# A two-layer diffusion backbone with product-key experts: scores issued one projection later, the shared bank's block fourth, five row buffers, fewer held activations, two adaLN groups moved between the layers

## The chip, the cores and the metric

The kernel runs on one core of one Trainium2 chip. The metric is the device time of one execution in microseconds; less is better. TensorE (PE in the profile) does the matrix products, with its weight loads shown apart as PEld; VectorE is DVE, ScalarE is ACT, GpSimd is POOL, and SyncE (SP) issues the plain DMAs. GpSimd issues the indirect DMAs, the gathers.

## What is computed

Latent tokens x (512 x 1024) and context tokens (256 x 1024) go through two layers. Each layer is three mixers side by side, a merge, and then an expert step (PEER) that picks 16 of 16384 experts for each of 8 heads of each token. Cut to what matters here:

```python
for l in range(2):
    mod = (silu(c) @ w_ada[l] + b_ada[l])          # adaLN: six rows of 1024 each
    h = modulate(rmsnorm(x, norm1_g[l]), mod[0], mod[1])
    q, k, v, zu, zv, zf, gl = split_cols(h @ w_in[l])
    x = x + mod[2] * mixer_merge(attention(q, k, v), chunk_mlp(zu, zv), fourier_mix(zf), gl, ...)
    h2 = modulate(rmsnorm(x, norm2_g[l]), mod[3], mod[4])
    x = x + mod[5] * peer_ffn(h2, ...)             # the context tokens alike in layer 0

def peer_ffn(t, w_q, sub_keys, u_tab, v_tab):
    q = rms_unit(t @ w_q)                          # 8 heads x 2 halves
    s = einsum('thpc,hpkc->thpk', q, sub_keys)     # key scores, 128 per half
    # top 16 of each half, of their 256 sums the top 16: idx (8 x 16 experts), weights g
    act = gelu(einsum('td,thkd->thk', t, u_tab[idx]))
    return einsum('thk,thkd->td', g * act, v_tab[idx])
```

## The kernel before

All data are float32. A product is made of three PE passes (`mm3`, lines 113 to 115): each operand is split into a high and a low half (ACT writes the high half at L102, DVE or POOL the low one at L109), and high times high, low times high and high times low are summed.

The expert step is done in two ways. **Dense**, for the 512 latent tokens of layer 0 and 384 of layer 1: all 16384 experts are computed in 128 chunks of 128 experts. `dense_u` multiplies a chunk of the u table (tile wH, wL) with the tokens into a PSUM bank du; a gelu on ACT (L972) puts the result into a held tile gS, or into DRAM (`gsd`) for chunks that are "spilled" and loaded back as gSr. `dense_v` loads the chunk of the v table (`vr`, by SP, three buffers with the tag vraw), splits it (vH, vL), multiplies gS by a table of gates (gt, L997), splits that (AH, AL) and multiplies it with eight 128-column blocks of v. Seven blocks accumulate over all chunks in PSUM banks da_0 to da_6. The eighth has no bank left: its product d goes into the one bank with the tag s, which du uses too, and DVE adds it to a tile da_7 in SBUF (L1013). A later du can start when this add has read the bank; d can start when gelu has read the du before it. NGSS says how many gS tiles are held, SPILL how many chunks go through DRAM. As many du as fit are made before the v chunks begin (`ahead`), the rest between them (`between`), one for each gS tile that comes free.

**Sparse**, for the two context blocks of layer 0 (128 tokens each) and the fourth latent block of layer 1: per block 128 gathers of rows of the u table (a job u), then 128 of the v table (a job v). A gather is issued by POOL (L869) into a tile `row` of a ring of LAG+1 = 4 buffers; `use` puts the work on DVE three steps later: for u a product with the tokens hn with its sum into dots (L888), for v a multiply-add into acc (L897). hn and acc share a buffer, so a u job loads hn (L887) after the acc of the job before has been stored. Steps are placed in the instruction stream by PE columns already issued (STEPS), so the jobs run beside the dense phase: in this trace c0 u from about 964 us, c0 v from 1694, c1 u from 2069, c1 v from 2501 to 2959 us. POOL also makes the wL halves of the u table.

At the end of layer 0 the eight da banks are scaled by mod, added to the residual (`xr`, four loads of 512 KB through the vraw buffers), stored (`xfin`), and their squares summed (vS); a product with ones (L294), a short chain on DVE (L172 to L181), a spread by a diagonal (dg, L299 and L305) and a copy (rf, L1282) give the norm factor with which layer 1 begins.

The adaLN rows are made by `ada` in groups: per group four loads `araw` (512 KB), 32 PE instructions as the trace counts them (L252), a copy, a small product and an add into mod. Groups 6 to 9 of layer 1 run beside its mixers.

`route1` makes the query of each head in two projections (tile pq), sums of squares (psq), the scores against the keys (pse) and the top 16 of them on DVE. The Tile framework's scheduler sets the order of the instructions on each engine.

Of the kernel before, what the change touches and what calls it, by code (L numbers as in the profile page):

```python
# [10 lines left out]
F32 = mybir.dt.float32  # L11
# [4 lines left out]
AF = mybir.ActivationFunctionType  # L16
# [5 lines left out]
P = 128  # L22
DEPTH = 2
D = 1024
# [7 lines left out]
NK = 128  # L32
# [16 lines left out]
LAG = 3  # L49
NGSS = (16, 30)  # L50
SPILL = ((40, 3), (40, 3))
FILL = (1.0, 1.3)
LEAD = 2
ADA = 6
# [23 lines left out]
class Ker:  # L78
# [156 lines left out]

    def ada(self, l, ccs, pool=None, tag="tl"):

        nc = self.nc
        sm, mod = self.lay[l]["sm"], self.lay[l]["mod"]
        p, nr = (pool, 4) if pool else (self.wp, self.wr)  # L240
        HW = 256
        for cc in ccs:
            acc = self.ps(tag)[:, :HW]
            for kk in range(4):
                raw = p.tile([P, D], F32, tag="wraw", name=self.nm("araw"), bufs=nr)
                nc.sync.dma_start(raw, self.a["wada"][l, cc, kk])
                self.spend()
                for j in range(2):
                    for hf in range(2):
                        q = 32 * (2 * j + hf)  # L250
                        c = j * 512 + hf * HW
                        nc.tensor.matmul(acc[q:q + 32, :], self.csil[:, 2 * kk + j, :], raw[:, c:c + HW],  # L252
                                         start=(kk == 0), stop=(kk == 3), skip_group_check=True)
                if tag == "fl" and kk < 3:
                    yield
            row = self.cp.tile([P, HW], F32, tag="row", name=self.nm("adar"), bufs=1)
            nc.scalar.activation(row, acc, AF.Copy)
            tp = self.ps(tag)
            for b in range(2):
# [336 lines left out]
    def merge_end(self, tmp, l, s, tag, e="alt"):  # L596
# [15 lines left out]
        for d in range(KD):  # L612
# [6 lines left out]
            yield  # L619
        nc.scalar.activation(s.r, self.rms(tmp, S, 1.0 / D, T), AF.Copy)  # L620

# [93 lines left out]
    def route1(self, l, tmp, rp, s, own=None):  # L715
# [5 lines left out]
        ss = rp.tile([P, nb, 16], F32, name=self.nm("pss"))  # L721
        self.rt = (V, I, ss)
        for h in range(HEADS):
            qs = []
            keys = tmp.tile([P, 2, NK], F32, tag="keys", name=self.nm("keys"), bufs=2)
            nc.sync.dma_start(keys, self.a["keys"][l, h])
            sp = self.ps("tl")
            for p in range(2):
                acc, = self.projT(l, W_PQ + 2 * h + p, [s], "pool", "px", own)
                q = tmp.tile([P, T], F32, tag=f"q{p}", name=self.nm("pq"), bufs=2)  # L730
                nc.scalar.activation(q, acc, AF.Copy)
                sq = tmp.tile([P, T], F32, tag="sq", name=self.nm("psq"), bufs=2)
                nc.scalar.activation(sq, acc, AF.Square)
                for b in range(nb):
                    nc.tensor.matmul(sp[:, 2 * b + p:2 * b + p + 1], sq[:, b * P:(b + 1) * P], self.onescol, start=True, stop=True)
                qs.append(q)
            nc.scalar.activation(ss[:, :, 2 * h:2 * h + 2], sp[:, :2 * nb].rearrange("p (a b) -> p a b", b=2), AF.Copy)
            for b in range(nb):
                sc = self.ps("tl")
                for p in range(2):  # L740
                    nc.tensor.matmul(sc[:, p * P:(p + 1) * P], qs[p][:, b * P:(b + 1) * P], keys[:, p, :], start=True, stop=True)
                sk = tmp.tile([P, 2, NK], F32, tag="s", name=self.nm("pse"), bufs=3)
                nc.scalar.activation(sk.rearrange("p a b -> p (a b)"), sc[:, :2 * P], AF.Copy)
                for p in range(2):
                    hp = 2 * h + p
                    s2 = tmp.tile([P, NK], F32, tag="s2", name=self.nm("ps2"), bufs=2)
                    self.top16(sk[:, p, :], s2, V[b][:, hp, :], I[b][:, hp, :])
            yield

    def route2(self, tmp, order, res, l=None):  # L750
# [106 lines left out]
    def step(self):  # L857
# [5 lines left out]
        if self.jobs:  # L863
            job = self.jobs[0]
            r, j, gp = job["r"], job["next"], self.gp
            if j == 0 and job["tab"] == "u":
                r["dots"] = gp.tile([P, P], F32, tag="dots", name=self.nm("dots"), bufs=2)
            row = gp.tile([P, D], F32, tag="row", name=self.nm("row"), bufs=LAG + 1)
            nc.gpsimd.indirect_dma_start(  # L869
# [107 lines left out]
    def dense_v(self, l, c, vp, sp, gS, gd, accs, acc7, between):  # L977
# [25 lines left out]
        def block(out, d, start, stop):  # L1003
            ds = slice(d * P, (d + 1) * P)
            self.mm3(out, vH[:, ds], vL[:, ds], AH, AL, start, stop)
        for d in range(4):
            block(accs[d], d, c == 0, c == NK - 1)
# [6 lines left out]
        self.added[c] = add.ins  # L1014
        for d in range(4, 7):
            block(accs[d], d, c == 0, c == NK - 1)
# [5 lines left out]
    def layer(self, l, xin, cin, xfin, rin):  # L1022
# [74 lines left out]
        with ExitStack() as e:  # L1097
# [10 lines left out]
            def context():  # L1108
# [4 lines left out]
                with ExitStack() as e2:  # L1113
                    tmp = self.pool(e2, f"cr{l}", side="right")
                    for b, r in enumerate(rc):
# [3 lines left out]
            self.interleave((mix(), 1), (context() if last else None, 1), (self.gates(gp, l, ss, (2, 1), PE2[l]), GATES[l]),  # L1119
                            (self.ada(l, range(ADA, 10) if last else range(4, 12), None, "fl"), 4 * AD[l]))  # L1120
            kvp = self.pool(ekv, f"kv{l}", side="right")
# [127 lines left out]
        with ExitStack() as e:  # L1249
            vp = self.pool(e, f"dv{l}")  # L1250
            acc7 = vp.tile([P, TD], F32, name=f"da{l}_7")
            with ExitStack() as e2:
# [11 lines left out]
                for c in range(NK):  # L1264
                    room[0] += not self.spilled(l, c)
                    self.dense_v(l, c, vp, op, gSs[c], gd, accs, acc7, between)
                known = not last and TD == SEQ
                if known:
                    S = vp.tile([P, SEQ], F32, tag="gSr", name=self.nm("vS"), bufs=2)
# [159 lines left out]
```

## Time and profile before

| | |
|---|---|
| median of 3 runs | 4845.99 us (4843.63 to 4858.48) |
| the profiled execution | 4854.88 us |
| its span in the profile | 4852.8 us |
| PE busy | 4484.0 us (92%) |
| DVE busy | 3251.8 us (67%) |
| POOL busy | 1794.6 us (37%) |
| mean granted clock of PE | 0.963 of full speed |

The span is the time from the first to the last instruction of the profiled execution; 2.1 us of that execution lie around it. Busy time is summed over stages that have different limits, so a change is read in its own stretch of the span.

### The profile page before, as it was taken

The numbers are of one execution on the slowest core, as the hardware profiler recorded it, in microseconds if no ns is written. First come the engines' busy times: TensorE is split into PE (matmuls) and PEld (weight loads), VectorE is DVE, ScalarE is ACT, GpSimd is POOL, SyncE is SP. The second block draws the span as 40 slices with busy tenths as digits, with TensorE's granted clock in tenths as the row PEclk, the third lists the DMA queues.
The fourth block names the chain that finished last, engine by engine and source line by source line (L and its number), as shares of the span: only waits on it lengthen the run. The fifth ranks groups of instructions, "written<-read, shape, count | busy, mean of one in ns | idle before, by whom it ended". The sixth has DMA issues, their size and how long they took to land.

```text
span 4852.8 us, 64913 instructions
## 1 busy us (share of the span) xinstructions
PE 4484.0 (92%) x23501; PEld 3843.0 (79%) x23501; DVE 3251.8 (67%) x6538; ACT 1872.6 (39%) x3456; POOL 1794.6 (37%) x1114
## 2 busy tenths in 40 slices
PE   7899988889889999999899989989898999999998
PEld 5678877767678788877778767767787899999998
DVE  3115586868996577766677874457459966777787
ACT  2223454333678322222222333334334883333332
POOL 1111012335323566655556420110224335555531
PEclk9999999989999999999999999999999999999999
DMA  4442345557768898988789886333536788888986
GB/s 167 137 145 78 95 124 171 179 187 229 238 237 283 291 316 307 319 274 281 264 299 305 308 270 206 97 102 108 176 89 197 265 280 282 293 290 301 309 281 227
DMA packets 447504, 1092.81 MB, mean 225 GB/s; under 512 B 37200, under 2 KB 193744, under 8 KB 440016
## 3 DMA queue, kind: packets, MB, share of 16 engines
q1 hardware_dynamic: 336592, 685.97, 43.4%
q0 software_dynamic: 110592, 402.70, 24.2%
q8 instruction: 185, 3.03, 0.3%
q14 instruction: 135, 1.11, 0.1%
HBM read 970.04 MB, written 118.49 MB: 224 GB/s over the span
## 4 chain that ended last, share of the span: by engine, by line
PE 43%; DMA 6%; DVE 6%; issue 6%; POOL 4%; ACT 1%; POOLq 0%; DVEq 0%; SPq 0%; ACTq 0%
PE da L114 5%; PE da L115 5%; PE da L113 5%; PE du L113 5%; PE du L115 5%; PE du L114 5%; POOL row L869 3%; DMA row<-in_u_dram,idxc 2%; PE ps L114 2%; PE ps L113 2%; PE ps L115 2%; PE px L952 1%; POOL wL L109 1%; DVE row L888 1%; PE d L113 1%
## 5 line engine op out<-in xcount | busy, mean ns | idle before, releaser
L109 POOL TENSOR_TENSOR wL<-wraw,wH 128x1024 fp32r<-128x1024 f32 x291 | 722.0, 2483 | 1138.5 <-ACT wH L102 1033.7
L102 ACT ACTIVATE wH<-wraw 128x1024 fp32r<-128x1024 f32 x460 | 486.7, 1059 | 1124.9 <-issue 311.1
L113 PE MATMUL du<-dH,wH 128*128 128x512 f32 (+1 forms) x2048 | 780.7, 381 | 71.3 <-DVE da L1013 47.2
L115 PE MATMUL du<-dH,wL 128*128 128x512 f32 (+1 forms) x2048 | 771.4, 377 | 44.6 <-DVE wL L109 24.4
L114 PE MATMUL du<-dL,wH 128*128 128x512 f32 (+1 forms) x2048 | 768.4, 375 | 2.4 <-DVE dL L336 2.4
L113 PE MATMUL da<-AH,vH 128*128 128x512 f32 (+1 forms) x1792 | 646.4, 363 | 7.0 <-ACT AH L102 7.0
L114 PE MATMUL da<-AL,vH 128*128 128x512 f32 (+1 forms) x1792 | 650.4, 363 | 1.4 <-DVE AL L109 1.2
L115 PE MATMUL da<-AH,vL 128*128 128x512 f32 (+1 forms) x1792 | 649.3, 362 | 0.0
L888 DVE SCALAR_TENSOR_TENSOR row<-row,hn 128x1024 f32<-128x1024 f32 x384 | 502.7, 1329 | 110.4 <-DMA row<-in_u_dram,idxc 93.4
L102 ACT ACTIVATE vH<-vr 128x1024 fp32r<-128x1024 f32 x256 | 271.8, 1062 | 776.8 <-PE da L114 552.7
L869 POOL DMA_INDIRECT row<-in_u_dram,idxc x256 | 329.4, 1287 | 528.9 <-DVE row L888 441.2
L897 DVE SCALAR_TENSOR_TENSOR acc<-row,dots,acc 128x1024 f32<-128x1024 f32 x381 | 502.0, 1318 | 10.0 <-DMA row<-in_v_dram,idxc 6.1
L113 PEld LDWEIGHTS du<-dH,wH 128*128 128x128 f32 x2048 | 399.4, 195 | 132.4 <-DVE da L1013 57.0
L869 POOL DMA_INDIRECT row<-in_v_dram,idxc x256 | 337.6, 1319 | 393.2 <-DVE acc L897 350.7
L115 PEld LDWEIGHTS du<-dH,wL 128*128 128x128 f32 x2048 | 398.7, 195 | 96.6 <-DVE wL L109 28.7
L114 PEld LDWEIGHTS du<-dL,wH 128*128 128x128 f32 x2048 | 399.3, 195 | 42.3 <-DVE dL L336 2.9
L1013 DVE TENSOR_TENSOR da<-d,da 128x512 f32<-128x512 f32 (+1 forms) x254 | 158.1, 623 | 333.4 <-PE d L115 333.0
L109 DVE TENSOR_TENSOR wL<-wraw,wH 128x1024 fp32r<-128x1024 f32 x169 | 213.9, 1266 | 249.4 <-ACT wH L102 220.3
L113 PEld LDWEIGHTS da<-AH,vH 128*128 128x128 f32 x1792 | 337.3, 188 | 43.3 <-ACT AH L102 8.2
L114 PEld LDWEIGHTS da<-AL,vH 128*128 128x128 f32 x1792 | 337.4, 188 | 39.0 <-DVE AL L109 4.2
L115 PEld LDWEIGHTS da<-AH,vL 128*128 128x128 f32 x1792 | 337.4, 188 | 35.0
L109 DVE TENSOR_TENSOR vL<-vr,vH 128x1024 fp32r<-128x1024 f32 x256 | 326.2, 1274 | 50.9 <-ACT vH L102 49.2
(390 smaller groups left out, 8968.1 us busy)
## 6 DMA issues: line engine op xcount, KB each, us to landing
wraw<-in_uT_dram SPq DMA_DIRECT2D x256, 512.0 KB, 4.6
vr<-in_v_dram SPq DMA_DIRECT2D x256, 512.0 KB, 6.2
wraw<-in_wt_dram SPq DMA_DIRECT2D x204, 512.0 KB, 3.9
gd<-stg SPq DMA_DIRECT2D x56, 1024.0 KB, 6.3
araw<-in_wada_dram SPq DMA_DIRECT2D x96, 512.0 KB, 4.6
gt<-gd SPq DMA_DIRECT2D x16, 2048.0 KB, 17.9
gt<-gd SPq DMA_DIRECT2D x16, 1536.0 KB, 12.3
gatex<-g SPq DMA_DIRECT2D x48, 256.0 KB, 2.1
```

The source lines that it names most:

```text
L102: nc.scalar.activation(H, src, AF.Copy)
L109: e.tensor_tensor(L, src, H.bitcast(F32), op=ALU.subtract)
L113: nc.tensor.matmul(out, aH, bH, start=start, stop=False)
L114: nc.tensor.matmul(out, aH, bL, start=False, stop=False)
L115: nc.tensor.matmul(out, aL, bH, start=False, stop=stop)
L869: nc.gpsimd.indirect_dma_start(out=row, out_offset=None, in_=self.a[f"{job['tab']}{job['l']}"], in_offset=bass.IndirectOffsetOnAxis(ap=r[" ...
L888: nc.vector.scalar_tensor_tensor(row, row, 1.0, job["hn"], op0=ALU.mult, op1=ALU.mult, accum_out=dots[:, j:j + 1])
L897: nc.vector.scalar_tensor_tensor(job["acc"], row, dots[:, j:j + 1], job["acc"], op0=ALU.mult, op1=ALU.add)
L952: nc.tensor.matmul(gp3[:, :, j], ob[:, j, :], oa[:, j, :], start=True, stop=True)
L1013: add = nc.vector.tensor_tensor(acc7, s[:, :TD], acc7, op=ALU.add)
```

## The change

- `NGSS` falls from 16 to 14 (layer 0) and from 30 to 27 (layer 1); `SPILL` rises from 40 to 42 chunks in both layers.
- The ring of row buffers grows from 4 to 5.
- In `dense_v` the block d is issued as the fourth of the eight instead of the fifth.
- adaLN groups 6 and 7 of layer 1 are no longer made beside layer 1's mixers, but at the end of layer 0's dense phase, ahead of the residual's loads, through the three vraw buffers and the one bank s.
- `merge_end` yields twice more and issues the two halves of the norm factor apart.
- In `route1` the sums, scores and top 16 of a head are issued after the first projection of the next head; one copy serves two token blocks.

```diff
-NGSS = (16, 30)
-SPILL = ((40, 3), (40, 3))
+NGSS = (14, 27)
+SPILL = ((42, 3), (42, 3))
...
-    def ada(self, l, ccs, pool=None, tag="tl"):
+    def ada(self, l, ccs, pool=None, tag="tl", ps=None, raws=("wraw", 4)):
...
-        p, nr = (pool, 4) if pool else (self.wp, self.wr)
+        p, rt, nr = (pool, *raws) if pool else (self.wp, "wraw", self.wr)
+        ps = ps or (lambda: self.ps(tag))
...
-            acc = self.ps(tag)[:, :HW]
+            acc = ps()[:, :HW]
...
-                raw = p.tile([P, D], F32, tag="wraw", name=self.nm("araw"), bufs=nr)
+                raw = p.tile([P, D], F32, tag=rt, name=self.nm("araw"), bufs=nr)
...
-        nc.scalar.activation(s.r, self.rms(tmp, S, 1.0 / D, T), AF.Copy)
+        yield
+        dg = self.rmsd(tmp, S, 1.0 / D, T)
+        yield
+        nc.scalar.activation(s.r, self.spread(dg, T), AF.Copy)
...
+        def best(h, keys, qs, sqs):
+
+            sp = self.ps("tl")
+            for p in range(2):
+                for b in range(nb):
+                    nc.tensor.matmul(sp[:, 2 * b + p:2 * b + p + 1], sqs[p][:, b * P:(b + 1) * P], self.onescol, start=True, stop=True)
+            nc.scalar.activation(ss[:, :, 2 * h:2 * h + 2], sp[:, :2 * nb].rearrange("p (a b) -> p a b", b=2), AF.Copy)
+            for b0 in range(0, nb, 2):
+                sc = self.ps("tl")
+                for j in range(2):
+                    for p in range(2):
+                        o = (2 * j + p) * P
+                        nc.tensor.matmul(sc[:, o:o + P], qs[p][:, (b0 + j) * P:(b0 + j + 1) * P], keys[:, p, :], start=True, stop=True)
+                sk = tmp.tile([P, 2, 2, NK], F32, tag="s", name=self.nm("pse"), bufs=2)
+                nc.scalar.activation(sk.rearrange("p j a b -> p (j a b)"), sc, AF.Copy)
...
                 acc, = self.projT(l, W_PQ + 2 * h + p, [s], "pool", "px", own)
+                if p == 0 and last is not None:
+                    best(*last)
...
-            row = gp.tile([P, D], F32, tag="row", name=self.nm("row"), bufs=LAG + 1)
+            row = gp.tile([P, D], F32, tag="row", name=self.nm("row"), bufs=LAG + 2)
...
-        for d in range(4):
+        for d in range(3):
             block(accs[d], d, c == 0, c == NK - 1)
         s = sp.tile([P, 512], F32, tag="s", name=self.nm("d7"))
         block(s[:, :TD], 7, True, True)
...
-        for d in range(4, 7):
+        for d in range(3, 7):
             block(accs[d], d, c == 0, c == NK - 1)
...
-                            (self.ada(l, range(ADA, 10) if last else range(4, 12), None, "fl"), 4 * AD[l]))
+                            (self.ada(l, range(ADA + 2, 10) if last else range(4, 12), None, "fl"), 4 * AD[l]))
...
+                shared = lambda: op.tile([P, 512], F32, tag="s", name=self.nm("s"))
+                if not last:
+                    self.drain(self.ada(l + 1, range(ADA, ADA + 2), vp, "tl", shared, ("vraw", 3)))
```

On PE, in one chunk of layer 0's dense phase, before (a number at the end of a name tells one tile from the next; the blocks are da_0 to da_6, the shared bank's block is d):

```order
L115 MATMUL da_2_14607<-AH_17984,vL_17978 128x512
L113 MATMUL da_3_14608<-AH_17984,vH_17977 128x512
L114 MATMUL da_3_14608<-AL_17985,vH_17977 128x512
L115 MATMUL da_3_14608<-AH_17984,vL_17978 128x512
L113 MATMUL d_3348_18000<-AH_17984,vH_17977 128x512
L114 MATMUL d_3348_18000<-AL_17985,vH_17977 128x512
L115 MATMUL d_3348_18000<-AH_17984,vL_17978 128x512
L113 MATMUL da_4_14609<-AH_17984,vH_17977 128x512
L114 MATMUL da_4_14609<-AL_17985,vH_17977 128x512
```

The same place after the change:

```order
L113 MATMUL da_2_14531<-AH_17953,vH_17948 128x512
L114 MATMUL da_2_14531<-AL_17954,vH_17948 128x512
L115 MATMUL da_2_14531<-AH_17953,vL_17949 128x512
L113 MATMUL d_3314_18005<-AH_17953,vH_17948 128x512
L114 MATMUL d_3314_18005<-AL_17954,vH_17948 128x512
L115 MATMUL d_3314_18005<-AH_17953,vL_17949 128x512
L113 MATMUL da_3_14532<-AH_17953,vH_17948 128x512
L114 MATMUL da_3_14532<-AL_17954,vH_17948 128x512
L115 MATMUL da_3_14532<-AH_17953,vL_17949 128x512
```

The three passes of d stand ahead of those of da_3, so three blocks lie between a chunk's du and d, and four between d and the next du.

On SP, at the end of layer 0, before:

```order
L985 DMA vr_23000<-in_v_dram 128x1024
L1272 DMA xr_23044<-xm_88 128x1024
L1272 DMA xr_23053<-xm_88 128x1024
L1272 DMA xr_23064<-xm_88 128x1024
L1278 DMA xfin_87<-xr_23044 128x1024
L1278 DMA xfin_87<-xr_23053 128x1024
L1272 DMA xr_23075<-xm_88 128x1024
L324 DMA nx_23168<-xfin_87 128x512
L324 DMA nx_23174<-xfin_87 128x512
```

After the change:

```order
L1003 DMA vr_22925<-in_v_dram 128x1024
L247 DMA araw_22969<-in_wada_dram 128x1024
L247 DMA araw_22975<-in_wada_dram 128x1024
L247 DMA araw_22981<-in_wada_dram 128x1024
L247 DMA araw_22987<-in_wada_dram 128x1024
L247 DMA araw_23001<-in_wada_dram 128x1024
L247 DMA araw_23007<-in_wada_dram 128x1024
L247 DMA araw_23013<-in_wada_dram 128x1024
L247 DMA araw_23019<-in_wada_dram 128x1024
L1293 DMA xr_23033<-xm_88 128x1024
L1293 DMA xr_23042<-xm_88 128x1024
L1293 DMA xr_23053<-xm_88 128x1024
```

Eight loads araw stand between the last load of the v table and the first residual load xr; all of them use the three buffers with the tag vraw in turn.

On DVE, in job c1 u beside the dense phase, before (a use is a row with hn; da_7 is the add that frees the shared bank):

```order
L109 TENSOR_TENSOR AL_18735<-gS_17105,AH_18734 128x512
L888 SCALAR_TENSOR_TENSOR row_18698,dots_17798<-row_18698,hn_17870 128x1024
L888 SCALAR_TENSOR_TENSOR row_18711,dots_17798<-row_18711,hn_17870 128x1024
L888 SCALAR_TENSOR_TENSOR row_18724,dots_17798<-row_18724,hn_17870 128x1024
L1013 TENSOR_TENSOR da_7_14601<-d_3480_18707,da_7_14601 128x512
L888 SCALAR_TENSOR_TENSOR row_18687,dots_17798<-row_18687,hn_17870 128x1024
L997 TENSOR_TENSOR gSr_18815<-gSr_18815,gt_18598 128x512
L109 TENSOR_TENSOR vL_18812<-vr_18809,vH_18811 128x1024
L109 TENSOR_TENSOR AL_18819<-gSr_18815,AH_18818 128x512
L1013 TENSOR_TENSOR da_7_14601<-d_3495_18789,da_7_14601 128x512
L888 SCALAR_TENSOR_TENSOR row_18769,dots_17798<-row_18769,hn_17870 128x1024
```

After the change, in the same job:

```order
L1031 TENSOR_TENSOR da_7_14525<-d_3445_18710,da_7_14525 128x512
L906 SCALAR_TENSOR_TENSOR row_18648,dots_17781<-row_18648,hn_17817 128x1024
L906 SCALAR_TENSOR_TENSOR row_18693,dots_17781<-row_18693,hn_17817 128x1024
L1015 TENSOR_TENSOR gS_17362<-gS_17362,gt_18522 128x512
L109 TENSOR_TENSOR vL_18778<-vr_18775,vH_18777 128x1024
L109 TENSOR_TENSOR AL_18783<-gS_17362,AH_18782 128x512
L906 SCALAR_TENSOR_TENSOR row_18718,dots_17781<-row_18718,hn_17817 128x1024
L1031 TENSOR_TENSOR da_7_14525<-d_3454_18755,da_7_14525 128x512
L906 SCALAR_TENSOR_TENSOR row_18704,dots_17781<-row_18704,hn_17817 128x1024
L906 SCALAR_TENSOR_TENSOR row_18730,dots_17781<-row_18730,hn_17817 128x1024
L906 SCALAR_TENSOR_TENSOR row_18766,dots_17781<-row_18766,hn_17817 128x1024
```

In the same job's start, on SP, the load of gt (2048 KB) now stands ahead of the load of hn, which it followed before. The uses on DVE still stand in runs of up to four between the work on a chunk, with an add into da_7 between them.

## Rows read from the trace of the kernel before

**Rows 1.** The page's busy time, share and instructions of each engine.

```profile
PE 4484.0 (92%) x23501; PEld 3843.0 (79%) x23501; DVE 3251.8 (67%) x6538; ACT 1872.6 (39%) x3456; POOL 1794.6 (37%) x1114
```

**Rows 2.** Windows: length; busy us of PE, PEld, DVE, ACT, POOL; clock; DMA.

```profile
850.00:1220.00 370.00, 326.77 (x1651) 263.24 (x1651) 287.98 (x1170) 119.46 (x209) 153.76 (x89) 0.93 0.61 198
1220.00:1680.00 460.00, 418.83 (x2296) 341.76 (x2297) 352.50 (x709) 307.25 (x764) 167.31 (x105) 0.96 0.76 264
1680.00:2090.00 410.00, 410.00 (x1811) 339.58 (x1810) 302.95 (x325) 118.94 (x152) 243.33 (x166) 1.00 0.91 310
2090.00:2505.00 415.00, 373.14 (x1560) 301.17 (x1559) 284.37 (x410) 103.72 (x129) 235.48 (x152) 0.96 0.83 272
```

**Rows 3.** Waits of PE from 2090 to 2520 us: total, times, longest.

```profile
PE du L113 <- DVE da L1013: 35.8, 15, 4.6
```

**Rows 4.** Waits of DVE from 2070 to 2505 us.

```profile
DVE row L888 <- DMA row<-in_u_dram,idxc: 55.1, 28, 5.2
...
DVE row L888 <- DMA hn<-hndc: 4.1, 1, 4.1
```

**Rows 5.** Waits of DVE from 1680 to 2070 us.

```profile
DVE acc L897 <- DMA row<-in_v_dram,idxc: 1.4, 2, 1.2
```

**Rows 6.** Timeline, 2207 to 2219 us: start, length, instruction [idle before].

```profile
2207.21 1.68 POOL L869 DMA_INDIRECT row<-in_u_dram,idxc  x1 [0.81 <-DVE row L888]
...
2208.00 1.22 DVE L888 SCALAR_TENSOR_TENSOR row<-row,hn 128x1024 f32<-128x1024 f32 x1
...
2209.19 1.98 POOL L869 DMA_INDIRECT row<-in_u_dram,idxc  x1 [0.30 <-issue]
...
2213.20 2.92 POOL L109 TENSOR_TENSOR wL<-wraw,wH 128x1024 fp32r<-128x1024 f32 x1 [0.78 <-ACT wH L102]
...
2217.45 1.23 DVE L888 SCALAR_TENSOR_TENSOR row<-row,hn 128x1024 f32<-128x1024 f32 x1 [3.58 <-DMA row<-in_u_dram,idxc]
```

**Rows 7.** DMA issues: KB each, median us to landing.

```profile
araw<-in_wada_dram SPq DMA_DIRECT2D x96, 512.0 KB, 4.6
gt<-gd SPq DMA_DIRECT2D x16, 2048.0 KB, 17.9
...
xr<-xm SPq DMA_DIRECT2D x4, 512.0 KB, 5.7
xfin<-xr SPq DMA_DIRECT2D x4, 512.0 KB, 4.7
```

**Rows 8.** Waits of PE from 850 to 1680 us.

```profile
PE tl L741 <- ACT pq L731: 1.6, 2, 0.8
```

**Rows 9.** Waits of PE from 4060 to 4853 us.

```profile
PE du L113 <- DVE da L1013: 11.4, 6, 3.0
```

**Rows 10.** Timeline of layer 1's dense phase from 4062 to 4065 us.

```profile
4062.52 1.06 ACT L102 ACTIVATE wH<-wraw 128x1024 fp32r<-128x1024 f32 x1 [3.26 <-PE du L114]
...
4063.49 0.47 ACT L972 ACTIVATE gS<-du 128x384 f32<-128x384 f32 x1
...
4063.84 0.19 PEld L113 LDWEIGHTS da<-AH,vH 128*128 128x128 f32 x1
...
4064.01 0.33 PE L113 MATMUL da<-AH,vH 128*128 128x384 f32 x1
```

**Rows 11.** Timeline of layer 0's end from 2820 to 2844 us.

```profile
2821.11 0.39 PE L115 MATMUL da<-AH,vL 128*128 128x512 f32 x1
...
2823.40 0.32 SPq L1272 DMA_DIRECT2D xr<-xm  x1
...
2829.57 0.75 DVE L1274 SCALAR_TENSOR_TENSOR xr<-da,mod,xr 128x512 f32<-128x512 f32 x1 [2.96 <-DMA xr<-xm]
...
2834.04 1.87 PE L294 MATMUL s<-onescol,vS 128*128 128x1 f32 x8 [12.54 <-DVE vS L283]
...
2841.20 2.05 PE L305 MATMUL s<-dg,ones 128*128 128x128 f32 x8 [5.29 <-DVE dg L299]
```

**Rows 12.** One line of the program: busy us, mean ns, idle before.

```profile
L252 PE MATMUL fl<-araw,csilp 128*32 128x256 f32 x768 | 81.0, 465 | 17.5 <-DMA araw<-in_wada_dram 14.3 <-PE tl L294 0.8 <-PE fl L260 0.7
```

More of the change, by code (lines that the diff above doesn't have):

```diff
@@ L257, in ada @@
             nc.scalar.activation(row, acc, AF.Copy)
-            tp = self.ps(tag)
+            tp = ps()
             for b in range(2):
@@ L722, in route1 @@
         self.rt = (V, I, ss)
+        def best(h, keys, qs, sqs):
[12 more added lines that the diff above has]
+                nc.scalar.activation(sk.rearrange("p j a b -> p (j a b)"), sc, AF.Copy)
+                for j in range(2):
+                    for p in range(2):
+                        hp = 2 * h + p
+                        s2 = tmp.tile([P, NK], F32, tag="s2", name=self.nm("ps2"), bufs=2)
+                        self.top16(sk[:, j, p, :], s2, V[b0 + j][:, hp, :], I[b0 + j][:, hp, :])
@@ L723, in route1 @@
+        last = None
         for h in range(HEADS):
-            qs = []
+            qs, sqs = [], []
             keys = tmp.tile([P, 2, NK], F32, tag="keys", name=self.nm("keys"), bufs=2)
             nc.sync.dma_start(keys, self.a["keys"][l, h])
-            sp = self.ps("tl")
             for p in range(2):
                 acc, = self.projT(l, W_PQ + 2 * h + p, [s], "pool", "px", own)
+                if p == 0 and last is not None:
+                    best(*last)
                 q = tmp.tile([P, T], F32, tag=f"q{p}", name=self.nm("pq"), bufs=2)
@@ L731, in route1 @@
                 nc.scalar.activation(q, acc, AF.Copy)
-                sq = tmp.tile([P, T], F32, tag="sq", name=self.nm("psq"), bufs=2)
+                sq = tmp.tile([P, T], F32, tag=f"sq{p}", name=self.nm("psq"), bufs=1)
                 nc.scalar.activation(sq, acc, AF.Square)
-                for b in range(nb):
-                    nc.tensor.matmul(sp[:, 2 * b + p:2 * b + p + 1], sq[:, b * P:(b + 1) * P], self.onescol, start=True, stop=True)
                 qs.append(q)
-            nc.scalar.activation(ss[:, :, 2 * h:2 * h + 2], sp[:, :2 * nb].rearrange("p (a b) -> p a b", b=2), AF.Copy)
@@ L738, in route1 @@
[L738 to L747, printed above, removed]
+                sqs.append(sq)
@@ L748, in route1 @@
+            last = h, keys, qs, sqs
             yield
+        best(*last)
+        yield
     def route2(self, tmp, order, res, l=None):
```

## The prediction

> **What bounds the kernel now.** The page's first line comes first: PE is busy for 92% of the span and no other engine for more than 67% [rows 1]. Time can therefore only come from the stretches in which PE doesn't run at its pace, so the table of windows is read next. From 1680 to 2090 us PE never stops: 410.00 us for 1811 matmuls at the full clock, 0.2264 us each, while the job c0 v and the dense chunks run side by side [rows 2]. In the next stretch, 2090 to 2505 us, the same dense chunks run beside the job c1 u, and only 1560 matmuls fit into 415 us [rows 2]. At 0.2264 us these are 353.2 us, so 61.8 us are lost: 415 - 373.1 = 41.9 us in which PE stood still, and 20 us in which it ran with less than the full clock (0.96 on average, against 1.00 before) [rows 2].
>
> What PE waits for there is in its list of waits: 35.8 us in 15 waits of du for the add of da_7, which has to read the shared bank first [rows 3]. The add comes late because DVE, which takes its work in order, stands at a use whose row hasn't landed: 28 such waits, 55.1 us together, 5.2 us at most [rows 4]. While c0 v ran it waited 1.4 us for rows [rows 5]. The timeline shows how one arises. A gather is issued when a use has freed a buffer; the one at 2209.19 followed its predecessor on POOL by 0.30 us and was generated for 1.98 us, and its use began at 2217.45, after 3.58 us of idleness [rows 6]. With four buffers, use n+4 can't be asked for before use n is done, and the uses come in runs of up to four.
>
> The two stretches ahead, in which latent routing and the first ahead-chunks run, leave PE idle for 43.2 of 370 us and 41.2 of 460 us [rows 2].
>
> **The change part by part.**
>
> *Five row buffers.* A gather may be issued one use earlier. The smallest lead that this gives is the length of one use inside a run, 1.22 us [rows 6]: 28 x 1.22 = 34 us of the 55.1, or 0.62 of it. Of the 61.8 us lost that is 38. The largest lead is a whole step of a job, 375 us / 128 = 2.9 us by the times of c0 v (1694 to 2069, with the kernel's description above), above the mean wait of 2.0 us; then nearly all row waits go, and what stays is the 4.1 us wait for hn [rows 4], which has 4.1 of 59.2 us: 57 us are gained. At the other end the buffer helps only where POOL is free to issue. It is in order as well, and a wL of 2.92 us stands between the gathers [rows 6]; if each wait hung on that, little would be left: I put this end at -5. I take -40, near the smaller lead, since the order on DVE still shows runs of four uses.
>
> What speaks against this term is that gathers might not be generated while DVE works. The gather at 2207.21 was generated in 1.68 us although a use began on DVE at 2208.00 and ran its usual 1.22 us [rows 6], so the term stays. [...]
>
> *hn.* In the changed order SP issues gt (2048 KB, 17.9 us to land [rows 7]) before c1 u's hn, instead of after it. DVE already waits 4.1 us for hn [rows 4]. 2048 KB at the 310 GB/s of the stretch before [rows 2] are 6.8 us, which hn may land later. Bounds 0 to +10 (with the lower clock after the stall); I take +4.
>
> *The fill stage.* c0 u shares the same ring in the stretches with 43 and 41 us of PE idleness [rows 2], but DVE is busy for 288 of 370 and 353 of 460 us there, and much of its work is routing, not uses. I take -5, with bounds -15 and +10; the latter for an order that the scheduler makes worse.
>
> *Scores behind the next projection, and merge_end.* In the routing stretches PE waits for a head's query 1.6 us in all [rows 8]; such heads come three times in the kernel. -2, bounds -4 and 0.
>
> *Block d as the fourth.* This gives the add of da_7 four blocks before the next du instead of three, and takes one block from the gelu ahead of d. In layer 1 a block is three passes of 0.17 us, 0.52 us. The gain: six waits for the add, 11.4 us in all [rows 9], each shortened by up to 0.52, is -3. The price: in layer 1 gelu ends at 4063.49 + 0.47 = 4063.96, while the weights of the fourth block are loaded from 4063.84 and its first pass starts at 4064.01 [rows 10]. So d, put there, finds the bank 0.12 us late. ACT has the wH of the next chunk (1.06 us) ahead of gelu [rows 10], so this repeats, for some 60 chunks: +7. Sum +4; bounds 0 (the load alone waits and PE catches up) and +17 (0.33 us each). In layer 0 the nine passes before the fourth block last 9 x 0.226 us [rows 2], 0.48 us longer than in layer 1, and d comes in time; the gain there is part of the ring's term, since the waits of [rows 3] are the same ones.
>
> *Fewer held tiles, two more chunks through DRAM.* Per layer two stores and two loads of at most 256 KB. At 310 GB/s [rows 2] that is 3.4 us of transfers, spread over hundreds of us, in which PE kept its pace with the DMA engines 0.91 busy [rows 2]. The number of chunks made ahead (SPILL + NGSS - LEAD) stays at 54 in layer 0 and falls from 68 to 67 in layer 1, the total is the same. The term is 0.
>
> *The two adaLN groups.* Their eight loads, PE work and copies go between layer 0's last product and the residual. Before, with T as the end of the last pass (2821.5), the fourth residual tile is loaded from 2823.40 and used at 2829.57, T + 8 [rows 11]; the others were in place. Then PE waits 12.54 us for the squares and 5.29 us for dg [rows 11]: nothing else covers this place, so what is late here is late at the end. After, all goes through three buffers. Three araw are in place at T. The fourth follows the first one's products (T + 0.6) and lands 4.6 us later [rows 7], at T + 5.2; the seventh follows the fourth, T + 5.7, and lands at T + 10.3; the residual tiles take over the buffers of the last three araw, the first at about T + 8, landing at T + 13.7 (5.7 us [rows 7]). It is scaled twice (1.5 us), stored (4.7 us [rows 7]), and only then the fourth residual tile can be loaded: T + 20, landing at T + 26. That is 18 us later than before; with the longer landings of a stretch in which gathers and weight loads run too I take 20. Given back is the groups' PE time in layer 1: 81.0 us over 24 groups [rows 12] is 3.4 each, -7. Sum +13. Bounds +3 (landings a third shorter, as when the queue is empty) and +26 (7 us for each of five landings in turn, nothing given back, since layer 1 waits for other things there).
>
> "DMA: Bandwidth & Descriptors", section "Anatomy of one DMA — SWDGE (gpsimd) path", of the Trainium skill fits a transfer as 2.0 us and bytes/436e3; an estimate from that page is 3.2 us for 512 KB, five in turn 16 us instead of 25, and the term would be +4. The trace's medians for these tiles are 4.6 to 5.7 us [rows 7], and they are used.
>
> **The sum.** -40 + 4 - 5 - 2 + 4 + 0 + 13 = -26 us, against the profiled execution's 4854.88 us. That one is 8.9 us above the median of the runs shown, 4845.99; I carry the difference over to the median: 4820. About 0.3%, 14.5 us, is what a measurement of this kernel can tell from no change.
>
> **Rivals.**
>
> *The ring gives little* (-15 in place of -40). Then POOL's order, not the buffers, sets when a row lands. For it: the gather at 2209.19 followed its predecessor by 0.30 us, so POOL was the limit there, and a wL of 2.92 us comes next [rows 6]. Its extreme is that the uses hold up the generation of the gathers; the ring then gives 0, the sum is +14 and the time 4860. Against both: in c0 v the same POOL work with the same ring went nearly without waits [rows 5]. Sum -1: 4845. [...]
>
> *More than that.* All row waits go (-57) and c0 u gains 15. For it: c0 v's stretch is the same dense work at full pace [rows 2]. Sum -57 + 4 - 15 - 2 + 4 + 13 = -53: 4793.
>
> *Slower: the chain between the layers.* Five transfers of 7 us in turn put the fourth residual tile at T + 35, +27, and layer 1 doesn't give back the 7. With the other terms (+4 - 5 - 2 + 4) that is +28 without the ring, so it decides against the change if the ring brings less than 13; with -10 there the time is 4864. For it: the place has no cover at all [rows 11]. Against it: the ring must nearly fail as well.
>
> **How the numbers follow.** The sum as forecast 0.50, the small ring 0.22 (0.03 of it for its extreme), the large one 0.14, slower 0.14. The first case has its own range of 4804 to 4834. Both its neighbours belong into the range; it ends at 4852 above, where the small ring with a longer chain lies, and at 4790 below: 4790 to 4852. Of the first case 0.44 lies beyond 0.3% on the fast side and 0.06 within; the large ring adds 0.14 to faster, the small one 0.03 to faster and 0.19 to within; the chain 0.01 to within and 0.13 to slower. So 0.61, 0.26 and 0.13.
>
> **What would show it.** In the changed kernel's trace, the job c1 u should last some 390 us instead of 432, the stretch should show about 0.2264 us per matmul outside a stall at its start for hn, and DVE's waits for rows should fall from 55 to below 20 us. At the end of layer 0 the wait of PE for vS, 12.54 us, should become about 25 or more with 64 records of ada ahead of it, and layer 1's mixers should be some 7 us shorter. In layer 1's dense phase d should wait for gelu by a tenth or two of a us in most chunks. The prediction is wrong if c1 u still waits for rows, if the residual's loads run ahead of the ada chain, or if those d waits reach half a us.

## The result

The changed kernel takes 4818.33 us (median of 7 runs, 4802.51 to 4823.92), the kernel before 4847.01 us (median of its 7 runs). The ratio is 0.9928 with a 95% interval of 0.9916 to 0.9941: faster by 0.7%, well beyond the 0.3% that a measurement can tell from no change. The forecast was 4820 us. The profiled execution took 4818.6 us, with a span of 4816.5 us against 4852.8 before, so the two traces differ by 36 us, and the medians by 29.

Read along the span, the two traces part where the forecast said, but not always by what it said. At layer 0's first product with the v table they are within 1 us of each other. The job c1 u is over 28.6 us earlier, layer 0's last dense product 30.8 us earlier. Then 15.5 us are given back before layer 1's first projection, some 11 are gained in the first stretch of layer 1's mixers, 1 is lost until layer 1's first product with the v table, and 10.8 are gained from there to the end. Some 4 to 8 of these last 10.8 us belong to this one execution: the stretch took 811.9 us here and 822.6 before, but 819.4 and 815.3 in the two runs of e3, which has the same code there.

**The stretch with c1 u.** The windows row of the changed kernel, in the columns of [rows 2]:

```profile
2090.00:2474.00 384.00, 360.88 (x1546) 293.19 (x1545) 277.69 (x402) 104.01 (x129) 234.89 (x149) 0.98 0.87 290
```

It holds 1546 matmuls in 384 us, 0.2484 us each; before it was 1560 in 415 us, 0.2660. The gathers of the job, by line and engine with shortest, median and longest duration in ns and first and last start, ran from 2069.0 to 2471.2 us (before to 2499.8):

```profile
L887 POOL DMA_INDIRECT row<-in_u_dram,idxc x128: 932/1440/1989, 2069.0 to 2471.2; - x128
```

PE's waits in this job, which answer to [rows 3]:

```profile
PE du L113 <- DVE da L1031: 22.4, 13, 3.7
```

and DVE's, which answer to [rows 4]:

```profile
DVE row L906 <- DMA row<-in_u_dram,idxc: 31.2, 18, 4.3
...
DVE row L906 <- DMA hn<-hndc: 5.2, 1, 5.2
```

The waits for rows fell from 55.1 us to 31.2, those for the add of da_7 from 35.8 to 22.4. The load of hn, now behind gt, landed in 10.2 us instead of 6.0, but DVE's wait for it is only 1.1 us longer. So the ring shortened the stalls but left more than half of the row waits.

**Between the layers.** The timeline of layer 0's end, which answers to [rows 11]:

```profile
2790.29 0.39 PE L115 MATMUL da<-AH,vL 128*128 128x512 f32 x1
...
2794.87 0.64 PE L253 MATMUL s<-araw,csilp 128*32 128x256 f32 x8 [2.76 <-DMA araw<-in_wada_dram]
...
2799.97 1.08 PE L253 MATMUL s<-araw,csilp 128*32 128x256 f32 x8 [1.19 <-DMA araw<-in_wada_dram]
...
2801.12 3.70 SPq L1293 DMA_DIRECT2D xr<-xm  x3
...
2805.00 1.02 PE L261 MATMUL s<-asel,adar 128*128 128x4 f32 x4 [0.56 <-ACT adar L258]
...
2811.74 0.36 SPq L1293 DMA_DIRECT2D xr<-xm  x1
...
2816.43 1.41 DVE L1295 SCALAR_TENSOR_TENSOR xr<-da,mod,xr 128x512 f32<-128x512 f32 x2 [1.17 <-DMA xr<-xm]
...
2819.55 1.84 PE L295 MATMUL s<-onescol,vS 128*128 128x1 f32 x8 [13.54 <-DVE vS L284]
...
2824.44 2.05 PE L306 MATMUL s<-dg,ones 128*128 128x128 f32 x8 [3.05 <-DVE dg L300]
...
2831.27 0.80 PE L113 MATMUL ps<-wH,hH 128*128 128x512 f32 x1 [1.30 <-ACT hH L336]
```

The last dense pass starts at 2790.29 and ends with T = 2790.7. The residual's fourth load is issued at 2811.74 and used at 2816.43, T + 25.7, where it was T + 8 before. PE still waits 13.5 us for the squares, now behind the 64 adaLN records: these and their waits for araw keep PE until T + 15.3, and the product of the squares starts at T + 28.9 instead of T + 12.5. Layer 1's first projection starts at 2831.27, T + 40.6; before it was T + 25.1 (2846.6 us). So the chain cost 15.5 us, less than the lengthening of 17.7 us that the fourth tile shows: the chain on DVE after the squares found no more v uses between its steps, and the wait for dg fell from 5.29 to 3.05 us.

**Layer 1's dense phase.** PE's waits there, which answer to [rows 9]:

```profile
PE du L113 <- DVE da L1031: 1.4, 1, 1.4
```

And the place of the block d in its timeline, which answers to [rows 10]:

```profile
4153.59 0.47 ACT L990 ACTIVATE gS<-du 128x384 f32<-128x384 f32 x1
...
4154.11 0.19 PEld L113 LDWEIGHTS d<-AH,vH 128*128 128x128 f32 x1 [0.16 <-ACT gS L990]
...
4158.24 0.19 PEld L113 LDWEIGHTS d<-AH,vH 128*128 128x128 f32 x1
```

Gelu ends at 4153.59 + 0.47 = 4154.06, and the load of d's weights begins 0.16 us late for it. In the next chunk, which has no du, it begins 4158.24 - 4154.11 = 4.13 us later. Over the phase the loads of d's weights waited for gelu 56 times (total, times, longest):

```profile
PEld d L113 <- ACT gS L990: 11.4, 56, 2.2
```

The waits of du for da_7 fell from 11.4 us in six to 1.4 in one.

### The profile page after: what moved, and what is told of

Same layout as the page of the kernel before. It is cut to its first block, busy times and chain, and to the rows that moved or that the text cites. A ratio compares the mean times of both kernels' runs of the same rounds, so it can differ in the third digit from the quotient of the medians.

```text
span 4816.5 us, 64853 instructions
## 1 busy us (share of the span) xinstructions
PE 4474.0 (93%) x23501; PEld 3843.9 (80%) x23501; DVE 3254.7 (68%) x6538; ACT 1861.6 (39%) x3416; POOL 1802.4 (37%) x1114
## 5 line engine op out<-in xcount | busy, mean ns | idle before, releaser
L887 POOL DMA_INDIRECT row<-in_u_dram,idxc x256 | 344.5, 1346 | 420.3 <-DVE row L906 321.1
L887 POOL DMA_INDIRECT row<-in_v_dram,idxc x256 | 325.6, 1272 | 383.6 <-DVE acc L915 344.6
L115 PEld LDWEIGHTS du<-dH,wL 128*128 128x128 f32 x2048 | 396.1, 193 | 85.7 <-POOL wL L109 25.1
L109 DVE TENSOR_TENSOR vL<-vr,vH 128x1024 fp32r<-128x1024 f32 x256 | 314.5, 1229 | 55.1 <-ACT vH L102 54.7
```

The source lines that it names most:

```text
L109: e.tensor_tensor(L, src, H.bitcast(F32), op=ALU.subtract)
L115: nc.tensor.matmul(out, aL, bH, start=False, stop=stop)
L887: nc.gpsimd.indirect_dma_start(out=row, out_offset=None, in_=self.a[f"{job['tab']}{job['l']}"], in_offset=bass.IndirectOffsetOnAxis(ap=r[" ...
```

## The experiments

All ratios are to the kernel before, run on the same chip. In e3 and e5 to e11 the two adaLN groups are made beside layer 1's mixers, as before; e3 is the base to which e5 to e10 are compared, and e11 is e3 run a second time. NGSS was lowered where a buffer needed room. The job c1 u is measured from its first to its last gather.

| run | ratio (95% interval) | c1 u, us | last dense pass to layer 1's first projection, us | first stretch of layer 1's mixers, us |
|---|---|---|---|---|
| before | 1 | 430.8 | 25.5 | 227.6 |
| after | 0.9928 (0.9916 to 0.9941) | 402.2 | 41.0 | 216.4 |
| e1, four row buffers | 1.0019 (1.0004 to 1.0035) | 435.5 | 40.6 | 219.6 |
| e2, ring only | 0.9930 (0.9905 to 0.9955) | 410.6 | 28.4 | 225.7 |
| e3, adaLN back | 0.9892 (0.9868 to 0.9916) | 400.8 | 28.1 | 215.3 |
| e4, d fifth | 0.9924 (0.9896 to 0.9952) | 403.6 | 41.8 | 217.5 |
| e5, old merge_end | 0.9870 (0.9853 to 0.9887) | 400.6 | 28.0 | 214.6 |
| e6, old route1 | 0.9910 (0.9893 to 0.9927) | 406.1 | 29.4 | 224.8 |
| e7, six row buffers | 0.9841 (0.9821 to 0.9861) | 390.4 | 28.9 | 215.4 |
| e8, own buffer for acc | 0.9856 (0.9838 to 0.9875) | 392.2 | 29.1 | 216.1 |
| e9, six and own | 0.9820 (0.9807 to 0.9834) | 381.0 | 30.4 | 215.8 |
| e10, seven row buffers | 0.9834 (0.9820 to 0.9847) | 386.1 | 30.6 | 214.4 |
| e11, e3 again | 0.9902 (0.9886 to 0.9918) | 400.7 | 29.8 | 216.8 |

The columns in us are read from one profile each, as differences between the starts of the first or last such instruction on PE (the chain from the start of the last dense pass); "first stretch" is from the first projection to the first product with the tag px.

**e1: four row buffers, all else as changed.**

```diff
-            row = gp.tile([P, D], F32, tag="row", name=self.nm("row"), bufs=LAG + 2)
+            row = gp.tile([P, D], F32, tag="row", name=self.nm("row"), bufs=LAG + 1)
```

> The changed kernel with four row buffers again, all else as changed. Theory (the ring is what c1 u gained by): the job c1 u takes about 430 us again instead of 402, DVE's waits for rows there return to about 55 us from 31, and the kernel is 28 us slower than the changed one, some 4847 us. Rival (the earlier block d and the other order on DVE brought it): c1 u stays near 405 us and the time near 4820.

Measured: 1.0019, slightly slower than before, and 0.9% slower than the changed kernel (44 us, where the theory had 28). The gathers of c1 u ran for 435.5 us, and DVE's waits in it are those of before:

```profile
L887 POOL DMA_INDIRECT row<-in_u_dram,idxc x128: 932/1439/1996, 2070.8 to 2506.3; - x128
```

```profile
DVE row L906 <- DMA row<-in_u_dram,idxc: 57.9, 18, 7.3
...
DVE row L906 <- DMA hn<-hndc: 5.8, 1, 5.8
```

The ring is what c1 u gained by; the other order on DVE and the earlier d alone don't help it. By its ratio the kernel stands 9 us above the kernel before, where the theory had it level with it: the chain between the layers is 15 us longer here too (40.6 us), and the first stretch of layer 1's mixers gives back only 8.

**e2: the kernel before with five row buffers.**

```diff
-NGSS = (16, 30)
-SPILL = ((40, 3), (40, 3))
+NGSS = (14, 27)
+SPILL = ((42, 3), (42, 3))
...
-            row = gp.tile([P, D], F32, tag="row", name=self.nm("row"), bufs=LAG + 1)
+            row = gp.tile([P, D], F32, tag="row", name=self.nm("row"), bufs=LAG + 2)
```

> The kernel before with five row buffers and the smaller NGSS and larger SPILL that make room for them, nothing else. Theory: c1 u gains its 28 us here too, the chain between the layers stays as before (25 us from the last dense product to layer 1's first), and the time is about 4818 us or a little less. Rival (the ring works only together with the block d a place earlier): half of it or less, 4832 or more.

Measured: 0.9930, all of the whole change's gain with one line of it and the memory for that line. c1 u took 410.6 us:

```profile
L869 POOL DMA_INDIRECT row<-in_u_dram,idxc x128: 935/1424/1988, 2057.6 to 2468.2; - x128
```

DVE's waits for rows in it were

```profile
DVE row L888 <- DMA row<-in_u_dram,idxc: 22.2, 17, 6.0
```

So everything else in the change sums to nothing, within the interval, which is 12 us either way here. The job c1 u gained 20 us, not the 28 of the theory. Of the 8 us that the changed kernel has more, 5 go with route1 (e6 against e3, below). As the row waits are 9 us less here than in the changed kernel, while the job is longer, they don't set its length alone.

**e3: the adaLN groups back beside layer 1's mixers.**

```diff
-                            (self.ada(l, range(ADA + 2, 10) if last else range(4, 12), None, "fl"), 4 * AD[l]))
+                            (self.ada(l, range(ADA, 10) if last else range(4, 12), None, "fl"), 4 * AD[l]))
...
-                if not last:
-                    self.drain(self.ada(l + 1, range(ADA, ADA + 2), vp, "tl", shared, ("vraw", 3)))
```

> The changed kernel with the two adaLN groups beside layer 1's mixers again. Theory: from the last dense product of layer 0 to layer 1's first projection 25 us instead of 41 (-15), layer 1's mixers 7 to 11 us longer; the sum is 4 to 8 us less than the changed kernel, 4811 to 4814 us. Rival (what layer 1 gained after it is not the adaLN groups'): the mixers keep their gain and the time is some 15 us less, 4803.

Measured: 0.9892, and 0.9902 (0.9886 to 0.9918) in a second run on another chip; against the changed kernel that is 13 to 17 us less. The rival was right. The chain is 28.1 us, near the 28.4 of e2, which has the ring alone, in the timeline of layer 0's end:

```profile
2782.25 0.39 PE L115 MATMUL da<-AH,vL 128*128 128x512 f32 x1
...
2794.34 1.87 PE L295 MATMUL s<-onescol,vS 128*128 128x1 f32 x8 [11.71 <-DVE vS L284]
...
2810.39 0.80 PE L113 MATMUL ps<-wH,hH 128*128 128x512 f32 x1 [2.24 <-ACT hH L336]
```

and the first stretch of layer 1's mixers isn't longer with the groups in it. Its windows row, and that of the changed kernel:

```profile
2810.00:3026.00 216.00, 211.35 (x1114) 169.41 (x1115) 115.45 (x190) 77.93 (x122) 18.37 (x17) 0.99 0.68 223
```

```profile
2831.00:3048.00 217.00, 207.24 (x1042) 169.46 (x1043) 119.67 (x190) 76.68 (x120) 23.56 (x21) 0.97 0.64 213
```

The changed kernel has 72 matmuls less there, yet takes a us more: 207.24 us of 217 busy, against 211.35 of 216. The 64 records of the two groups take 5.7 us in e3. Without them PE is idle for 5.1 us more (9.8 against 4.7), and its other matmuls take 1.6 us longer, at a granted clock of 0.97 instead of 0.99. So what the groups no longer fill is lost again, mostly as waits. PE's waits there in e3:

```profile
PE tl L113 <- ACT fo L705: 1.8, 2, 1.1
```

and in the changed kernel:

```profile
PE tl L113 <- ACT fo L705: 5.8, 2, 5.2
PE tl L295 <- DVE nr L284: 1.8, 1, 1.8
```

Whether the groups had filled these waits, or the chain made them, isn't settled: in the changed kernel 21 gathers of c1 v are still issued after layer 1's first projection, in e3 17, so that more uses stand on DVE there.

For the second run of the same kernel (e11) this was expected:

> The changed kernel with the adaLN groups beside layer 1's mixers once more, for a comparison with the others on one chip: 0.987 to 0.9895.

Its 0.9902 lies just above that.

**e4: the block d as the fifth again.**

```diff
-        for d in range(3):
+        for d in range(4):
             block(accs[d], d, c == 0, c == NK - 1)
...
-        for d in range(3, 7):
+        for d in range(4, 7):
             block(accs[d], d, c == 0, c == NK - 1)
```

> The changed kernel with the block d as the fifth again. Theory: in layer 1 each chunk with a du loses the 0.14 us that it now waits for gelu (6 to 8 us less in all), the waits of du for the add of da_7 grow by up to 0.5 us each in layer 1 (3 us more) and by 0.7 us each in c1 u (13 waits, 9 us more): within 5 us of the changed kernel, 4815 to 4823. Rival (d as the fourth is what shortened layer 1's dense phase by 11 us): 4829 or more.

Measured: 0.9924, the same as with d fourth. c1 u took 403.6 us, so d's place isn't part of its gain. In layer 1's dense phase the waits of du for da_7 are back:

```profile
PE du L113 <- DVE da L1031: 7.9, 5, 1.8
```

and the weights of d hardly wait for gelu any more, where the changed kernel has 56 such waits:

```profile
PEld d L113 <- ACT gS L990: 3.7, 2, 3.4
```

The time from one d to the next says what the place costs. Where nothing is lost it is 4.16 us for a chunk without a du (24 matmuls) and 8.32 for one with a du (48). What comes on top, where it is less than 0.5 us, sums to 9.0 us in the changed kernel (52 times 0.14 us) and to 3.4 with d fifth, so the place costs 5.6 us. Against it stand the 6.5 us of waits that the changed kernel doesn't have. The two nearly cancel.

**e5 and e6: merge_end and route1 as before, each alone, on e3.** All earlier runs with the changed forms of both show a shorter first stretch of layer 1's mixers; e2 and the kernel before don't. In e5 the norm factor is issued in one piece:

```diff
-        yield
-        dg = self.rmsd(tmp, S, 1.0 / D, T)
-        yield
-        nc.scalar.activation(s.r, self.spread(dg, T), AF.Copy)
+        nc.scalar.activation(s.r, self.rms(tmp, S, 1.0 / D, T), AF.Copy)
```

> The changed kernel with the adaLN groups beside layer 1's mixers again and with the norm factor of merge_end issued in one piece, as before. It tells where the 10 us come from by which layer 1's first stretch (from its first projection to its first attention product) is shorter in every run with the changed merge_end and route1 (215 to 220 us) than in those without (226 to 228 us). Theory A (merge_end): 226 us here, and the kernel 10 us slower than without this edit, ratio about 0.991. Theory B (route1): 215 us, ratio 0.989.

In e6 route1's inner part is that of the kernel before (the diff of route1 above, the other way round).

> The same base (adaLN groups beside layer 1's mixers), with the scores of route1 issued with their own head again. Theory A (merge_end): layer 1's first stretch 215 us, ratio about 0.989. Theory B (route1): 226 us and a ratio of about 0.991. Also, SP's order at the start of c1 u has hn ahead of gt again: if hn behind gt costs what was forecast (4 us), the job c1 u is some 4 us shorter than 401 us.

Measured: e5 0.9870 with a first stretch of 214.6 us, e6 0.9910 with 224.8 us. Theory B: it is route1 that gains the 10 us (9.5 against e3), and not where it stands, but in the mixers of the next layer. In the whole time the gain is less sharp: e6 is 19 us slower than e5 on the same chip, but only 4 to 9 us slower than the two runs of e3 on others, with intervals that overlap. The same stretch in e6, windows and waits:

```profile
2819.00:3046.00 227.00, 215.70 (x1120) 172.44 (x1121) 113.71 (x188) 78.26 (x122) 15.77 (x15) 0.98 0.64 207
```

```profile
PE tl L113 <- ACT fo L705: 3.1, 2, 2.8
PE tl L922 <- DVE rx L923: 2.8, 1, 2.8
...
PE tl L295 <- DVE nr L284: 2.2, 1, 2.2
```

PE waits 2.8 us for rx and 2.2 us for nr there, and runs at 0.98 of the clock, against 0.99 and neither wait in e3. rx is the context's residual, which follows the end of the job c1 v; its first product comes to PE 125.4 us after layer 1's first projection in e6, and 131.5 us after it in e3. The jobs' steps are placed by PE columns already issued, so code that moves in route1 moves the steps of all later jobs, and with them the residual. That link is argued from the code; the waits are shown. As to hn: in e6 SP has it ahead of gt, and c1 u was 5 us longer than in e3, not shorter.

Whether merge_end's two yields do harm is open: e5 is at 0.9870, but it ran on another chip than e3, whose two ratios are 0.9892 and 0.9902, and its interval overlaps both of theirs.

**e7, e8, e9 and e10: what is left in c1 u.** On e3, six row buffers; five with a buffer of its own for acc; both; and seven.

```diff
-NGSS = (14, 27)
+NGSS = (12, 24)
...
-            row = gp.tile([P, D], F32, tag="row", name=self.nm("row"), bufs=LAG + 2)
+            row = gp.tile([P, D], F32, tag="row", name=self.nm("row"), bufs=LAG + 3)
```

> The same base with six row buffers (NGSS 12 and 24 make room). Theory (each buffer gives the gathers a lead of one use, and about 31 us of row waits are left in c1 u): those waits fall below 15 us, c1 u from 401 to about 388 us, ratio 0.986. Rival (what is left is POOL's own order: gathers behind wL and behind each other): c1 u 396 to 404 us, ratio 0.989.

```diff
-NGSS = (14, 27)
+NGSS = (12, 24)
...
-            job["acc"] = self.gp.tile([P, D], F32, tag="hn", name=self.nm("acc"))
+            job["acc"] = self.gp.tile([P, D], F32, tag="acc", name=self.nm("acc"))
```

> The same base, five row buffers, with a buffer of its own for acc, so that c1 u's hn no longer waits for the store of c0 v's acc (NGSS 12 and 24 make room). Theory (the start of c1 u costs DVE 5 us and PE about 10 us with the lower clock): the wait for hn goes, c1 u 8 to 12 us shorter, ratio 0.987. Rival (the stall is made up by the slack behind it): c1 u within 4 us of 401 us, ratio 0.989.

> The changed kernel with the adaLN groups beside layer 1's mixers, six row buffers and a buffer of its own for acc (NGSS 10 and 21 make room). Theory (the two waits in c1 u are apart, so their gains add): c1 u without row waits and without the wait for hn, some 382 us, ratio 0.981. Rival (with six buffers the start's stall is made up behind it): 0.984, as with six buffers alone.

> The same base with seven row buffers (NGSS 10 and 21). Theory (with six buffers only 6 us of row waits are left in c1 u): no more than 5 us better than six, ratio 0.983 to 0.984.

DVE's waits for rows and hn in c1 u with six buffers (e7):

```profile
DVE row L906 <- DMA hn<-hndc: 7.3, 1, 7.3
DVE row L906 <- DMA row<-in_u_dram,idxc: 6.2, 8, 1.6
```

with an own buffer for acc (e8):

```profile
DVE row L906 <- DMA row<-in_u_dram,idxc: 24.4, 16, 3.3
```

and with both (e9):

```profile
DVE row L906 <- DMA row<-in_u_dram,idxc: 3.1, 3, 1.1
```

Six buffers nearly end the row waits, and c1 u takes 390.4 us. The rival, that POOL's order sets them, falls. With an own buffer for acc the hn load is issued long before, and the wait at the start is gone: 392.2 us. Together 381.0 us, 20 us below e3, of 10.4 and 8.6 apart: they add. Seven buffers gave 0.9834, no more than six. e9, at 0.9820, is the fastest version here, 1.1% less time than the changed kernel by the ratios; part of that may come from the smaller NGSS, since layer 0's first product with the v table then comes earlier (1629.9 us in e7, 1633.0 in e8, 1615.6 in e9, 1645.1 in e3). e7 as a whole is 25 to 30 us below e3, of which c1 u has 10. No run has the smaller NGSS alone, so the ratios of e7 to e10 don't tell what a buffer is worth; the lengths of c1 u and the waits in it do better.

## Why the prediction was right

The forecast of 4820 us met 4818. Its mechanism was right: c1 u's row waits were the gain, the chain between the layers the main loss. Five terms were off, and they made up for each other; that the two numbers meet within 2 us is luck.

Some of the prediction's own signs came out against it. It was to be wrong if c1 u still waits for rows, and c1 u does, for 31.2 us where below 20 were forecast; it lasts 402 us instead of 390, and behind its start (2110 to 2474 us) a matmul takes 0.2456 us, not 0.2264. And PE's wait for the squares was to become 25 us or more: it is 13.5, since PE came to it only at T + 15.3. Layer 1's mixers are 11 us shorter, not 7, but by e3 and e6 through route1 and not through the groups. That d waits for gelu by a tenth or two of a us in most chunks with a du was right.

- **The ring** (-40, and +4 for hn): c1 u gained 28.6 us. Without the ring, all else as changed, it is 4.7 us longer than before (e1), so the ring is worth 33 us there; alone it gives 20 (e2). The term was too large, because I took a lead of 1.22 us for every wait, as if all were of the mean length: 34 of 55.1 us. In the trace of the kernel before, 13 of the 28 waits are shorter than that; 1.22 us or the whole wait, whichever is less, sums to 25.1 us and leaves 30.0, and 31.2 stayed. By the same share of the 61.8 us lost, 25.1 us make 28. The +4 for hn behind gt was 1.1 us in the trace, and e6, which has the old order, gives no sign of a cost. Of the 20 us that I put down to the lower clock in this stretch, the 0.96 of its row makes only 15.
- **The small ring's extreme**, that the uses hold up the generation of the gathers and the ring brings 0, is not what happens. In c1 u of the changed kernel 76 of the 128 gathers ran beside a use for more than 0.1 us and were generated in 1.38 us on average, the other 52 in 1.34; and a fifth and a sixth buffer took the row waits from 57.9 (e1) to 31.2 (after) and 6.2 us (e7), while DVE went on with the same uses. The Trainium skill, "SBUF — State Buffer", section "SBUF: two separate sides", says that GpSimd can't write descriptors while VectorE runs an instruction in a 2-port perf mode. The trace doesn't show the mode of a use; the durations show no such stop.
- **The chain between the layers** (+20): 15.5 us in the traces, 13 between e3 and the changed kernel. The fourth residual tile came at T + 25.7, where the sum of landings said T + 26, but its parts were off and made up for each other: the sixth araw took 7.7 us to land instead of 4.6, so that the first residual load was issued at T + 10.4 instead of T + 8, and the three landings behind it took 13.7 us instead of 16.1. The 2 us that I added for longer landings were not there, and the tail behind the squares was 2 us shorter. The fit of the Trainium skill's "DMA: Bandwidth & Descriptors", section "Anatomy of one DMA — SWDGE (gpsimd) path", is given there for DMAs that GpSimd issues, while SP issued these; the 3.2 us that I estimated from it were too little for the 3.7 to 7.7 us of these landings.
- **What layer 1 gives back** (-7): nothing, by e3. The groups' 5.7 us are there, but I counted them as if PE had nothing else to wait for; in the changed kernel it waits for fo (5.8 us).
- **route1** (-2): about 10 us in its stretch, by e6, and not in the routing but in layer 1's mixers. I looked only at the waits where the code stands, and the edit also moved the places of the jobs' steps.
- **Block d as the fourth** (+4): 0, by e4. The price was right in kind and near in size, 0.16 us late for gelu in the timeline and 5.6 us in all instead of 7; the gain was 6.5 us instead of 3. I read this as waits that don't arise at all where the add is on time once, so that one block's 0.52 us takes away more than its own length; no run shows it.
- **The fill stage** (-5) and the spilled chunks (0): c0 u's last gather came 2.5 us earlier. Its first comes at 967.4 to 979.4 us in four runs with the same code up to there (after, e1, e3, e4), so a gain of 5 us can't be told.

## What to carry to other kernels

A ring of buffers for gathers is to be sized by the waits of its consumer, not by how busy that is: one more buffer alone gave as much as the whole change, on an engine that was busy for two thirds of the span. Price it wait by wait, since a lead can't shorten a wait by more than the wait's own length. Work that is moved costs time at a place without cover, and may give nothing back where it stood: look for the wait that comes up when it is gone. Where the order of later work is set by counts of what was issued before, an edit's effect may stand a layer away from the edit, and its own waits don't show it.

## What the runs showed of the hardware that was not expected

Gathers of 128 rows of 4 KB were generated in 0.93 to 2.00 us each throughout c1 u. The median was 1.44 us in the kernels with four, five, six and seven buffers alike (e1, after, e7, e10), and 1.17 us in two others, with four (before) and five (e4). So the larger number of gathers that may be under way didn't slow the generation; what makes the two medians is not known.
